# A fused two-layer trunk: attention from the first chunk to the last, with the other products in one even sequence

## The chip, the core and the metric

The kernel runs on one core of a Trainium2 chip. A core has a matrix engine (TensorE, PE in the profile; its weight loads are shown apart as PEld), three engines for element-wise work (VectorE or DVE, ScalarE or ACT, GpSimd or POOL), and SyncE (SP), which here issues nearly all DMA transfers between the device's memory and the core's own. Each engine takes its instructions in one fixed order; where one needs another engine's result, it waits at the head of its engine's queue, and what stands behind it waits too. The metric is the time of one execution on the device in microseconds (us), lower is better.

## The reference, cut to what matters

Two layers over a sequence of 2048 tokens with 1024 channels. Layer A is a pooling mixer; layer B is the attention that the change is about. Cut to layer B:

```python
kv_in = rms_norm(x, kv_norm)
k_all, v_all = jnp.split(kv_in @ w_kv, 2, axis=-1)
k_sh = rms_norm(split_heads(k_all), k_norm); v_sh = split_heads(v_all)
h = rms_norm(x, b_norm[j])
q, z = jnp.split(h @ b_w_in[j], 2, axis=-1)
q = rms_norm(split_heads(q), b_q_norm[j])          # 16 heads of 64
o = stick_breaking_attention(q, k_sh, v_sh)        # a[t,s] = beta[t,s] * prod_{s<i<t} (1 - beta[t,i]), s < t
x = x + (o * jax.nn.silu(z)) @ b_w_out[j]
x = x + (p[i] @ ple_w[i]) * jax.nn.sigmoid(x @ ple_gate_w[i])
```

beta is the sigmoid of the scaled logits. The product over the tokens between s and t is a scan along the keys, so attention is causal and has no softmax. The products of layer B outside attention are z (1024 to 1024), the output projection, the gate and the small per-layer embedding.

## The kernel before

Tokens are cut in four chunks of 512. The first `with` block computes layer A and q, k and v of layer B for chunks 0 to 3 in turn, and leaves q, k, v and the residual x2 in device memory. Every fp32 number that goes through a matmul is held as a pair, a rounded part and the rest, and a product of two pairs is three matmuls (high by high, high by low, low by high). The halves of x2 are kept in memory too (x2p), for chunks 0 to 2; those of chunk 3 are still on the core when they are wanted.

The second `with` block is attention with the rest of layer B woven in. Its work is a list of slots `(c, h, kc)`: query chunk c, head h, key chunk kc. The list goes through c = 3, 2, 1, 0, for each c through 16 heads, for each head through kc = c down to 0: 64, 48, 32 and 16 slots. Each slot has four steps, one per 128 queries in `front` and one per 128 keys in `turn` and `gather`, 640 steps in all:

- `front`: two matmuls for the logits (L790, L791), a sigmoid on ACT (L794), and the scan on DVE (L799 where kc = c, which is the diagonal and has 128 to 512 keys; L802 elsewhere, always 512).
- `turn`, six steps later: up to four transposes (L815), a cast on ACT (L818) and the low half on DVE (L819).
- `gather`, eight steps later: two matmuls with v (L827, L828). After a head's last one its 64 rows are copied and added (L832, L833); after every second head four ACT instructions add the ends (L839) and POOL multiplies by the stored z gate (L840).

`begin` loads q, k and v of the next slot at the first step of each slot; q, k and v share ten buffers of the pool `io`. The order of slots is written out by hand; within it the framework's planner fixes each engine's order by the program's order and its own estimate of times. `keep_in_program_order` pins an instruction behind all that was written before it on its engine.

The other products are a generator, the filler, that is advanced by a rate at every step; each `next` gives one 128x512 matmul (`piecewise`, L856, L858, L860). `gate_z(c)` makes z of one chunk (8 output tiles of 24 matmuls) and stores silu(z) (DVE L889, ACT L891, POOL L892, store L893). `post(c)`, called the rest below, is the output projection (L913 to L916), the gate, the embedding and the final store (L935 to L948); it needs all heads of chunk c. `pair_up` turns a finished pair of heads into its two halves (L868, L869), which `post` multiplies. Beside attention of chunk 3 run the z of chunks 3, 2, 1, 0; beside chunk 2 the rest of chunk 3; beside chunk 1 that of chunk 2; beside chunk 0 that of chunk 1. Last, without attention, comes the rest of chunk 0. The rate is set anew at each joint of chunks:

```python
rate = POSTZ / 64.0 - AHEAD * LAG_T / 256.0        # beside chunk 3
rate = POST / (64.0 * c3 - 2 * LAG_G)              # beside chunk c3 - 1
```

which is 2.91, 2.51, 3.94 and 9.19 pieces a step; the second form is spent 16 steps before its chunk's last.

Of the kernel before, what the change touches and what calls it, by code (L numbers as in the profile page):

```python
# [34 lines left out]
def trunk_kernel(ctx, tc, x, p, a_norm, a_w_in, a_w_group, a_scale, a_w_out, kv_norm, w_kv,  # L35
# [28 lines left out]
    x2p = [[dram.tile([P, 2, W5], F32, name=f"x2p{s}_{o}") for o in range(KT)] for s in range(NSUB - 1)]  # L64
# [114 lines left out]
    with ExitStack() as st:  # L179
# [316 lines left out]
        def run_g(s, b, wg, wl):  # L496
# [13 lines left out]
            for k in range(2):  # L510
# [4 lines left out]
                if s + 1 < NSUB:  # L515
                    nc.sync.dma_start(out=x2p[s][o], in_=f(pr))
# [231 lines left out]
    with ExitStack() as st:  # L748
# [16 lines left out]
        kcount = [0]  # L765

# [55 lines left out]
        def gather(st, kt):  # L822
# [6 lines left out]
            if st["last"] and kt == 3:  # L829
                half, os, c, h2 = st["h"] % 2, st["os"], st["c"], st["h"] // 2  # L830
                mine, other = slice(half * HD, (half + 1) * HD), slice((1 - half) * HD, (2 - half) * HD)
                A.copy(out=os[mine], in_=po[other])  # L832
                V.tensor_tensor(out=os[mine], in0=po[mine], in1=os[mine], op=ALU.add)  # L833
                if half:
                    zt = t2.tile([P, W5], F32, tag="zt", name="zt", bufs=1)
                    nc.sync.dma_start(out=zt, in_=zd[c][h2])
                    for j in range(4):
                        js = slice(j * P, (j + 1) * P)
                        A.activation(out=os[:, js], in_=os[:, js], func=AF.Identity, bias=ends[c][:, h2, j : j + 1])  # L839
                    G.tensor_tensor(out=os, in0=os, in1=zt, op=ALU.mult)  # L840
                    outs[c].append(os)

        tail = [0]
# [9 lines left out]
        def piecewise(ps, units, acts, c0):  # L853
            n = len(acts)
            for kt in range(n):
# [4 lines left out]
                T.matmul(ps, wst(units, kt, 1, c0), acts[kt][:, 0], start=False, stop=(kt == n - 1))  # L860
                yield

        def pair_up(c):

            if len(ogs[c]) < len(outs[c]):
                os = outs[c][len(ogs[c])]
                pr = pair("og")
                A.copy(out=pr[:, 0], in_=os)  # L868
                V.tensor_tensor(out=pr[:, 1], in0=os, in1=f(pr[:, 0]), op=ALU.subtract)  # L869
                ogs[c].append(pr)  # L870

        def gate_z(c):

            xs = chunk[c]["x2"] if c == NSUB - 1 else []
            for o in range(len(xs), KT):
                pr = pair("xz")
                nc.sync.dma_start(out=f(pr), in_=x2p[c][o])
                xs.append(pr)
# [5 lines left out]
            for o in range(KT):  # L884
                wz = early.pop("w") if "w" in early else stored(wzd[o])
                ps = dense()
                yield from piecewise(ps, wz, xs, 0)
                zr = t2.tile([P, W5], F32, tag="tmp", name="zr", bufs=4)
                V.tensor_tensor(out=zr, in0=ps, in1=rb, op=ALU.mult)  # L889
                sg = t2.tile([P, W5], F32, tag="tmp", name="sgz", bufs=4)  # L890
                A.activation(out=sg, in_=zr, func=AF.Sigmoid)  # L891
                G.tensor_tensor(out=zr, in0=zr, in1=sg, op=ALU.mult)  # L892
                nc.sync.dma_start(out=zd[c][o], in_=zr)  # L893
                if c == 0:
                    pair_up(NSUB - 1)

        POSTZ = 8 * 24
        POST = 8 * 24 + 8 * 30 + 9

        def post(c):  # L900
# [4 lines left out]
            while len(og) < 8:  # L905
                pair_up(c)
            for o in range(KT):
# [7 lines left out]
                A.copy(out=pr[:, 0], in_=xr)  # L915
                G.tensor_tensor(out=pr[:, 1], in0=xr, in1=f(pr[:, 0]), op=ALU.subtract)  # L916
                x3.append(pr)
            pt_ = []
# [8 lines left out]
            yield  # L927
            late = []
            for o in range(KT):
# [5 lines left out]
                A.activation(out=sg, in_=ps, func=AF.Sigmoid)  # L935
                pl = dense()
                yield from piecewise(pl, wl, pt_, 0)
                V.tensor_tensor(out=sg, in0=pl, in1=sg, op=ALU.mult)
                (V if tail[0] else G).tensor_tensor(out=sg, in0=sg, in1=f(x3[o][:, 1]), op=ALU.add)
                V.tensor_tensor(out=sg, in0=sg, in1=f(x3[o][:, 0]), op=ALU.add)  # L940

                def finish(o=o, sg=sg):
# [12 lines left out]
                if c:  # L955
                    pair_up(c - 1)
                yield
            late.pop()()
# [106 lines left out]
```

## Time and profile before

| | us |
|---|---|
| median of 3 runs | 2773.11 (2772.43 to 2773.38) |
| the profiled execution | 2771.59 |
| its span, first to last instruction | 2768.5 |
| first logits of attention | at 1364.04 |
| end of attention's last matmul | at 2660.84 |

The span is what the profile's times are counted in. An engine's busy time is the union of its instructions. A line of a group gives the source line, engine, operation, output and inputs, shapes and count, then busy time and the mean in nanoseconds of one, then idle time before it and what ended that. A line of a table by stretches gives the stretch and its length, then the busy time and count of PE, PEld, DVE, ACT and POOL, the granted clock of TensorE as a share of the full one, the mean busy share of the DMA engines, and their GB/s; for one source line alone it has only the engines which that line runs on.

### The profile page before, as it was taken

To read this page: it belongs to the slowest core of one execution; us is meant where nothing else is said; L and a number is where in the kernel's file an instruction comes from. 1 tells how busy PE (TensorE), PEld (TensorE's weight loads), DVE (VectorE), ACT (ScalarE), POOL (GpSimd) and SP (SyncE) were. 2 spreads that over 40 slices of the span, in tenths; PEclk is the share of its full clock that TensorE was granted. 3 is DMA by queue.
4 is the path that set the end of the run, shared out by engine and by line. 5 is a ranking of instruction groups with operands and counts; after the bars stand their busy time and mean duration, and the time that the engine had idled before them with its cause. 6 is when DMAs were issued, how large, how long until landed. Compare 5 with 4: busy or idle time off the path is not lost. (4 is left out here: it accounts for less than half of the span.)

```text
span 2768.5 us, 39557 instructions
## 1 busy us (share of the span) xinstructions
PE 2725.8 (98%) x13715; PEld 2259.8 (82%) x13715; DVE 1962.6 (71%) x2573; ACT 1385.6 (50%) x2801; POOL 871.2 (31%) x695
## 2 busy tenths in 40 slices
PE   9999999999999999999999999999999999999999
PEld 7888888888888888888878888887878778878877
DVE  6767535655357544565499999999999998996642
ACT  5445532445234552345356566566666666564431
POOL 2575338542475325753121111111110011102120
PEclk9999999999999999999999999999999999999999
DMA  8655695647946489444678565556555565668765
GB/s 290 237 189 177 218 335 195 224 147 254 342 151 231 162 255 310 134 149 169 194 251 284 173 218 171 164 168 189 162 160 166 181 191 186 199 185 265 240 206 160
DMA packets 335835, 573.21 MB, mean 207 GB/s; under 512 B 32462, under 2 KB 166638, under 8 KB 335636
## 3 DMA queue, kind: packets, MB, share of 16 engines
q1 hardware_dynamic: 330186, 563.03, 62.3%
q10 hardware_dynamic: 5450, 7.66, 0.9%
q8 instruction: 108, 1.77, 0.3%
q14 instruction: 91, 0.75, 0.1%
HBM read 430.01 MB, written 132.19 MB: 203 GB/s over the span
## 5 line engine op out<-in xcount | busy, mean ns | idle before, releaser
L536 PE MATMUL psd<-wpair,x 128*128 128x512 f32 x2304 | 543.8, 393 | 0.0
L818 ACT CAST at<-psa 128x512 fp32r<-128x512 f32 (+3 forms) x640 | 333.6, 522 | 403.1 <-PE psa L815 397.5
L802 DVE TENSOR_TENSOR_SCAN pp<-kap,pp,zeros 128x512 f32<-128x512 f32 x384 | 507.9, 1324 | 4.9 <-ACT kap L794 4.4
L536 PEld LDWEIGHTS psd<-wpair,x 128*128 128x128 f32 x2304 | 428.1, 188 | 86.2
L819 DVE TENSOR_TENSOR at<-psa,at 128x512 fp32r<-128x512 f32 (+3 forms) x640 | 379.9, 595 | 76.5 <-ACT at L818 73.2
L815 PE MATMUL psa<-ident,pp 128*128 128x128 f32 x2176 | 346.1, 274 | 19.3 <-DVE at L819 17.3
L794 ACT ACTIVATE kap<-psl 128x512 f32<-128x512 f32 (+3 forms) x640 | 344.7, 539 | 10.2 <-PE psl L791 9.3
L815 PEld LDWEIGHTS psa<-ident,pp 128*128 128x128 f32 x2176 | 263.8, 140 | 95.2 <-DVE at L819 38.4
L790 PE MATMUL psl<-kk,qa 128*128 128x512 f32 (+3 forms) x640 | 280.3, 438 | 0.4 <-ACT kap L794 0.4
L828 PE MATMUL pso<-at,vv 128*128 128x512 f32 (+3 forms) x640 | 235.5, 368 | 0.0
L827 PE MATMUL pso<-at,vv 128*128 128x512 f32 (+3 forms) x640 | 233.7, 365 | 0.7 <-ACT at L818 0.6
L791 PE MATMUL psl<-kk,qb 128*128 128x512 f32 (+3 forms) x640 | 233.7, 365 | 0.0
L799 DVE TENSOR_TENSOR_SCAN pp<-kap,ahead 128x128 f32<-128x128 f32 (+3 forms) x256 | 226.7, 887 | 6.0 <-ACT kap L794 4.7
L131 PE MATMUL psd<-xp,wpair 128*128 128x512 f32 x512 | 201.7, 395 | 1.9 <-ACT xp L269 1.4
L132 PE MATMUL psd<-xp,wpair 128*128 128x512 f32 x512 | 200.5, 392 | 0.0
L133 PE MATMUL psd<-xp,wpair 128*128 128x512 f32 x512 | 200.0, 391 | 0.0
L113 DVE SCALAR_TENSOR_TENSOR wpair<-wraw,gains,wpair 128x512 fp32r<-128x512 f32 x192 | 170.4, 908 | 37.5 <-ACT wpair L112 36.1
L892 POOL TENSOR_TENSOR zr<-zr,sgz 128x512 f32<-128x512 f32 x32 | 62.2, 1944 | 383.0 <-ACT sgz L891 305.6
L108 POOL TENSOR_TENSOR wpair<-wraw,wpair 128x512 fp32r<-128x512 f32 x99 | 146.0, 1489 | 60.2 <-ACT wpair L106 60.2
L112 ACT ACTIVATE wpair<-wraw,gains 128x512 fp32r<-128x512 f32 x192 | 134.7, 719 | 58.9 <-PE psd L536 32.9
L827 PEld LDWEIGHTS pso<-at,vv 128*128 128x128 f32 x640 | 120.2, 188 | 27.4 <-ACT at L818 1.6
L828 PEld LDWEIGHTS pso<-at,vv 128*128 128x128 f32 x640 | 120.3, 188 | 24.7
(211 smaller groups left out, 5396.4 us busy)
## 6 DMA issues: line engine op xcount, KB each, us to landing
kk<-kd SPq DMA_DIRECT2D x320, 128.0 KB
vv<-vd SPq DMA_DIRECT2D x160, 256.0 KB
wraw<-in_w_kv_dram SPq DMA_DIRECT2D x128, 256.0 KB
wpair<-wzd SPq DMA_DIRECT2D x64, 512.0 KB
wpair<-wod SPq DMA_DIRECT2D x64, 512.0 KB
wpair<-wgd SPq DMA_DIRECT2D x64, 512.0 KB
wpair<-wu SPq DMA_DIRECT2D x48, 512.0 KB
wpair<-wi SPq DMA_DIRECT2D x36, 512.0 KB
```

What stands on the lines that cost most here:

```text
L131: T.matmul(ps, wst(units, kt, 0, c0), acts[kt][:, 0], start=(begin and kt == order[0]), stop=False)
L536: T.matmul(pss2[i], ck["x2"][kt][:, xh, tk], wst(ws, kt, wh, 0, W5), start=(kt == 0 and xh == 0 and wh == 0), stop=(kt == KT - 1 and wh == 1))
L790: T.matmul(ps[:, :w], qa[:, qs], kk[:, :w], start=True, stop=False)
L791: T.matmul(ps[:, :w], qb[:, qs], kk[:, :w], start=False, stop=True)
L794: A.activation(out=kp[:, r0:], in_=ps[:, :w], func=AF.Sigmoid, scale=-1.0)
L799: V.tensor_tensor_scan(out=pp[:, r0:][:, ::-1], data0=kp[:, r0:][:, ::-1], data1=ahead[:, r0:][:, ::-1], initial=1.0, op0=ALU.mult, op1=AL ...
L802: V.tensor_tensor_scan(out=pp[:, ::-1], data0=kp[:, ::-1], data1=zeros.to_broadcast([P, W5]), initial=st["carry"][j], op0=ALU.mult, op1=AL ...
L815: T.transpose(pt[:, j * P : (j + 1) * P], pp[:, r0 + kt * P : r0 + (kt + 1) * P], ident)
L818: A.copy(out=at[:, 0, cs], in_=pt[:, cs])
L819: V.tensor_tensor(out=at[:, 1, cs], in0=pt[:, cs], in1=f(at[:, 0, cs]), op=ALU.subtract)
L827: T.matmul(po[:, cs], vv[:, kt, :], at[:, 0, cs], start=(st["diag"] and kt == 0), stop=False)
L828: T.matmul(po[:, cs], vv[:, kt, :], at[:, 1, cs], start=False, stop=(st["last"] and kt == 3))
```

## The change

1. The slots go through c = 0, 1, 2, 3. The first q and k that are loaded early are those of chunk 0.
2. There is one filler for the whole of attention: z of chunks 0, 1, 2, the rest of chunk 0, z of chunk 3, the rest of chunks 1 and 2. The rest of chunk 3 comes last, without attention. Its rate has two values, one for diagonal steps and one for the others, worked out over all 640 steps so that 20 pieces remain at the end.
3. All four chunks' x2 halves are stored and loaded again: those of chunk 0 before attention begins, those of chunks 1 and 2 behind the last output tile of the z before, those of chunk 3 at the end of the rest of chunk 0.
4. Late issue: `soon(k, fn)` puts an instruction k steps later in the program. It is used for the copy, the sum and the gate after a head, for the sigmoid and the gate of z, for the halves in `pair_up` and `post`, and for the gate's sigmoid and last sum in `post`; most of the ACT instructions among these are pinned in program order (`stay`). After attention everything is issued at once again.

The diff, cut to its core:

```diff
-    x2p = [[... for o in range(KT)] for s in range(NSUB - 1)]
+    x2p = [[... for o in range(KT)] for s in range(NSUB)]
...
+    def load_x2(c, o):
+        pr = pair("xz")
+        nc.sync.dma_start(out=f(pr), in_=x2p[c][o])
+        return pr
...
-                early["q"] = load_q(NSUB - 1, 0)
-                early["k"] = [load_k(NSUB - 1, 0), load_k(NSUB - 2, 0)]
+                early["q"] = load_q(0, 0)
+                early["k"] = [load_k(0, 0), load_k(0, 1)]
+                early["x"] = [load_x2(0, o) for o in range(KT)]
...
+        due, now, tail = [], [0], [0]
+        def soon(k, fn):
+            if tail[0]:
+                fn()
+                return lambda: None
+            item = (now[0] + k, len(due), fn)
+            due.append(item)
+            def force():
+                if item in due:
+                    due.remove(item)
+                    fn()
+            return force
...
+        def stay(ins):
+            return ins if tail[0] else tc.keep_in_program_order(ins)
...
-                A.copy(out=os[mine], in_=po[other])
-                V.tensor_tensor(out=os[mine], in0=po[mine], in1=os[mine], op=ALU.add)
+                soon(1, lambda: stay(A.copy(out=os[mine], in_=po[other])))
+                soon(2, lambda: V.tensor_tensor(out=os[mine], in0=po[mine], in1=os[mine], op=ALU.add))
+                if half:
+                    soon(3, gated)
+                    soon(6, lambda: outs[c].append(os))
...
+                follows = o == KT - 1 and c < 2
+                def behind(kt):
+                    early.setdefault("x", []).append(load_x2(c + 1, kt))
+                yield from piecewise(ps, wz, xs, 0, behind if follows else None)
...
+                def silu(o=o, zr=zr):
+                    sg = t2.tile([P, W5], F32, tag="tmp", name="sgz", bufs=4)
+                    stay(A.activation(out=sg, in_=zr, func=AF.Sigmoid))
+                    G.tensor_tensor(out=zr, in0=zr, in1=sg, op=ALU.mult)
+                    nc.sync.dma_start(out=zd[c][o], in_=zr)
+                    gates.add((c, o))
+                soon(1, silu)
...
-        def beside(c):
-            if c < NSUB - 1:
-                yield from post(c + 1)
-                return
-            for cz in range(c, -1, -1):
-                yield from gate_z(cz)
+        def beside():
+            for c in range(NSUB - 1):
+                yield from gate_z(c)
+            yield from post(0)
+            yield from gate_z(NSUB - 1)
+            for c in range(1, NSUB - 1):
+                yield from post(c)
...
-        for c in range(NSUB - 1, -1, -1):
+        for c in range(NSUB):
...
-        rate = POSTZ / 64.0 - AHEAD * LAG_T / 256.0
+        SPARE = 20
+        nd = sum(4 for c, h, kc in slots if kc == c)
+        on_diag = 3.1
+        off_diag = (4 * POSTZ + 3 * POST - SPARE - AHEAD * LAG_T - on_diag * nd) / (4 * len(slots) - nd + LAG_G)
...
-            owed += rate + (AHEAD if n < LAG_T else 0)
+            owed += on_diag if i < len(slots) and slots[i][2] == slots[i][0] else off_diag
+            owed += AHEAD if n < LAG_T else 0
...
+        settle()
+        pair_up(NSUB - 1)
+        settle()
+        for _ in filler:
+            settle()
         tail[0] = 1
-        for _ in post(0):
+        for _ in post(NSUB - 1):
             pass
```

More of the change, by code (lines that the diff above doesn't have):

```diff
@@ L867, in pair_up @@
                 pr = pair("og")
-                A.copy(out=pr[:, 0], in_=os)
-                V.tensor_tensor(out=pr[:, 1], in0=os, in1=f(pr[:, 0]), op=ALU.subtract)
+                stay(A.copy(out=pr[:, 0], in_=os))
+                soon(1, lambda: V.tensor_tensor(out=pr[:, 1], in0=os, in1=f(pr[:, 0]), op=ALU.subtract))
                 ogs[c].append(pr)
         def gate_z(c):
[L874 to L878, printed above, removed]
+            xs = early.pop("x")
             ps = (psl if "w" in early else psa).tile([P, 4, P], F32, tag="psl" if "w" in early else "psa", name="psar")
@@ L914, in post, with halves @@
                 pr = pair("x3")
[L915 to L916 removed]
+                def halves(pr=pr, xr=xr):
+                    stay(A.copy(out=pr[:, 0], in_=xr))
+                    G.tensor_tensor(out=pr[:, 1], in0=xr, in1=f(pr[:, 0]), op=ALU.subtract)
+                made = soon(1, halves)
                 x3.append(pr)
+                if o < 2 and c < NSUB - 1:
+                    pair_up(c + 1)
             pt_ = []
@@ L927, in post @@
             yield
+            made()
             late = []
```

65 lines of the change are left out of this document (32 added, 33 removed).

## The prediction

> **What bounds the kernel now.** I read the page first: the shares of the engines.
>
> ```profile
> span 2768.5 us, 39557 instructions
> ## 1 busy us (share of the span) xinstructions
> PE 2725.8 (98%) x13715; PEld 2259.8 (82%) x13715; DVE 1962.6 (71%) x2573; ACT 1385.6 (50%) x2801; POOL 871.2 (31%) x695
> ```
>
> PE looks busy throughout. But a matmul is shown from its start to a modelled end, and ends overlap the next starts (a case stands below), so 98% may hide a PE that works below its pace. So next comes the table of stretches, cut where a new chunk's first logits (L790) start: chunks 3, 2, 1, 0, and then the end without attention.
>
> ```profile
> 1364.00:1864.60 500.60, 496.73 (x2706) 414.03 (x2705) 472.02 (x564) 298.94 (x598) 79.06 (x44) 1.00 0.64 204
> 1864.60:2219.60 355.00, 344.12 (x1917) 283.31 (x1916) 344.22 (x434) 226.80 (x468) 38.93 (x25) 1.00 0.55 172
> 2219.60:2480.80 261.20, 255.09 (x1409) 212.38 (x1408) 235.47 (x305) 156.25 (x338) 34.39 (x24) 1.00 0.60 190
> 2480.80:2660.80 180.00, 174.24 (x940) 145.55 (x939) 121.90 (x190) 91.92 (x220) 32.15 (x24) 1.00 0.76 241
> 2660.80:2768.50 107.70, 100.88 (x461) 82.51 (x460) 24.90 (x36) 17.90 (x32) 11.59 (x9) 0.99 0.55 176
> ```
>
> After the colon pair and the length come PE, PEld, DVE, ACT, POOL, the clock, the DMA share and GB/s. Attention takes 2660.8 - 1364.0 = 1296.8 us for 256 + 192 + 128 + 64 = 640 steps. The clock is full throughout, so it plays no part. DVE is at 94, 97, 90 and 68%: the stages have different limits. That is the opening for an even mix.
>
> The same table for the products' first matmul (L856) alone shows stretches that have almost none:
>
> ```profile
> 1863.50:1876.50 13.00, 0.00 (x0) 0.19 (x1) 1.00 0.60 186
> 2204.10:2232.30 28.20, 0.00 (x0) 0.01 (x1) 1.00 0.52 164
> 2466.80:2493.60 26.80, 0.79 (x2) 0.38 (x2) 1.00 0.56 171
> 2639.10:2660.80 21.70, 1.81 (x5) 0.94 (x5) 1.00 0.59 188
> ```
>
> They are the joints between chunks, 89.7 us in sum, in which PE has attention's own work only. The rate leaves 16 steps empty before each joint and 8 steps drain after it.
>
> Then the stretches between the joints, whole heads of chunks 3, 2, 1 and 0 (144, 144, 96 and 32 steps), for all engines, and in the second fence for L856:
>
> ```profile
> 1428.80:1706.90 278.10, 278.10 (x1526) 232.98 (x1525) 263.95 (x317) 168.93 (x339) 42.04 (x23) 1.00 0.70 222
> 1893.30:2160.20 266.90, 262.42 (x1464) 218.29 (x1462) 260.77 (x328) 170.06 (x351) 32.12 (x20) 1.00 0.53 168
> 2249.20:2450.90 201.70, 199.77 (x1099) 167.52 (x1097) 180.17 (x232) 118.57 (x255) 29.18 (x20) 1.00 0.61 195
> 2517.00:2615.10 98.10, 98.10 (x524) 83.41 (x522) 62.29 (x94) 46.14 (x109) 20.14 (x15) 1.00 0.80 255
> ```
>
> ```profile
> 1428.80:1706.90 278.10, 55.37 (x140) 26.32 (x140) 1.00 0.70 222
> 1893.30:2160.20 266.90, 47.01 (x118) 22.17 (x118) 1.00 0.53 168
> 2249.20:2450.90 201.70, 49.03 (x123) 23.12 (x123) 1.00 0.61 195
> 2517.00:2615.10 98.10, 38.24 (x96) 18.07 (x96) 1.00 0.80 255
> ```
>
> Every product matmul comes in threes (L856, L858, L860), so the stretches hold 420, 354, 369 and 288 of them, and steps of 1.931, 1.853, 2.101 and 3.066 us. What one costs PE is its start to the next start:
>
> ```profile
> 2717.11 0.60 PE L945 MATMUL psao<-ident,sg 128*128 128x128 f32 x4
> 2717.46 0.47 PE L856 MATMUL psdt<-x,wpair 128*128 128x512 f32 x1
> 2717.77 0.39 PE L858 MATMUL psdt<-x,wpair 128*128 128x512 f32 x1
> 2718.00 0.39 PE L860 MATMUL psdt<-x,wpair 128*128 128x512 f32 x1
> ```
>
> 2717.77 to 2718.00 is 0.23 us for a product; four transposes and a product, 2717.11 to 2717.77, take 0.66, so a transpose takes 0.108.
>
> **The sum for PE.** In the stretches of chunks 3 and 0 PE is busy all the time, so what is left after the products is attention's own need. Chunk 3: (278.1 - 420 x 0.23) / 144 = 1.260 us a step. Chunk 0, all steps on the diagonal, with about 24 transposes of rest: (98.1 - 66.2 - 2.6) / 32 = 0.916. So a step off the diagonal takes (4 x 1.260 - 0.916) / 3 = 1.375. Chunk 2 then needs (0.916 + 2 x 1.375) / 3 = 1.222, chunk 1 1.146. One z is 192 products, 44.2 us; one rest is 432 products and 40 transposes, 103.7 us or 0.2346 for each of its 442 pieces. All of it: 256 x 0.916 + 384 x 1.375 + 4 x 44.2 + 3 x 103.7 = 1250 us. The attention part took 1296.8, so 47 us are the most that any order can win.
>
> **The sum for DVE.** Its own work per step is what stands in the stretch less the products' share, from the groups of the chunk 3 stretch and, in the second fence, of the chunk 0 stretch:
>
> ```profile
> L889 DVE TENSOR_TENSOR zr<-psd,rb 128x512 f32<-128x512 f32 x18 | 12.0, 666 | 0.6 <-issue 0.6
> ...
> L869 DVE TENSOR_TENSOR og<-os,og 128x512 fp32r<-128x512 f32 x2 | 1.3, 676 | 0.0
> ```
>
> ```profile
> L940 DVE TENSOR_TENSOR sg<-sg,x 128x512 f32<-128x512 f32 x5 | 4.5, 907 | 6.9 <-POOL sg L939 6.9
> L913 DVE TENSOR_TENSOR xr<-psd,xr 128x512 f32<-128x512 f32 x6 | 4.1, 677 | 0.6 <-issue 0.6
> L938 DVE TENSOR_TENSOR sg<-psd,sg 128x512 f32<-128x512 f32 x5 | 3.4, 674 | 0.8 <-PE psd L860 0.8
> L869 DVE TENSOR_TENSOR og<-os,og 128x512 fp32r<-128x512 f32 x4 | 2.6, 676 | 2.6 <-ACT og L868 2.6
> L925 DVE TENSOR_TENSOR ple<-psap,ple 128x512 fp32r<-128x512 f32 x2 | 1.3, 666 | 0.0
> ```
>
> In chunk 0's stretch 15.9 us go with 288 products, 0.055 each; a z with one og per 24 products comes to 2 x 0.67 / 24 = 0.056, the same. Own work a step: chunk 3 (263.95 - 13.3) / 144 = 1.740; chunk 2 260.77 / 144 - 0.135 = 1.676; chunk 1 1.877 - 0.211 = 1.666; chunk 0 1.947 - 0.495 = 1.452.
>
> **The change, part by part.** (1) Order and rate. 3.1 pieces go to a diagonal step, and (768 + 1326 - 20 - 24 - 3.1 x 256) / (640 - 256 + 8) = 3.205 to the others, with 24 extra in the first six steps. The chunks mix them to 3.1, 3.153, 3.170 and 3.179. PE a step (0.23 a piece in chunks 0 and 1, 0.233 and 0.2346 in 2 and 3): 1.629, 1.871, 1.961, 2.006. DVE a step (0.055 a piece): 1.62, 1.84, 1.85, 1.915. In chunks 0 and 1 both are level. Chunk 2's old stretch was so too: PE 1.222 + 354 / 144 x 0.23 + 0.02 = 1.81, DVE 1.811, and a step took 1.853, that is 1.023 of the greater. I add that 2.3% in chunks 0 and 1, and nothing in 2 and 3, since chunk 3's old stretch held PE at 278.10 of 278.10 with DVE at 95%. Sum: 64 x 1.667 + 128 x 1.914 + 192 x 1.961 + 256 x 2.006 + 24 x 0.23 = 1247 us. Then 8 draining steps, at the old end's 21.7 / 16 = 1.36 us, 10.9, and the 20 pieces kept back, 4.7, under which the last head's chain lies. Attention 1263 against 1297: -34 us. The part after it stays at 107.7: the same 432 products, for chunk 3 in place of 0.
>
> (2) Eight more stores of x2 halves, in chunk 3's first layer, and eight more loads, 512 KB each: 4.2 MB each way. Cover: in the window 1050 to 1130, in the midst of that, PE is full:
>
> ```profile
> 1050.00:1130.00 80.00, 80.00 (x355) 66.23 (x354) 39.46 (x50) 20.47 (x38) 53.16 (x51) 1.00 0.75 260
> ```
>
> I take nothing; at the window's 260 GB/s with a share of 0.75, some 347 GB/s at a full share, the 4.2 MB would be 12 us if the cover were gone. The next z's halves are loaded behind each product step of the last column, 21 pieces or 6 steps ahead; z of chunk 3 gets its own as the halves before it are freed. Nothing, with 2 us as the upper end for one late first load.
>
> (3) Late issue: copies, sums and gates of attention go one to six steps back in ACT, DVE and POOL order, so that none stands at the head of its queue with its input not made. Gain: nothing to the 1% idle in chunk 1's old stretch, some 2.5 us over that chunk; loss: os and the logits' output bank are held two steps longer, nothing to 2 us in chunk 0, where a head has only four steps. I take nothing.
>
> (4) SP. In chunk 0 every slot is a new head and needs seven loads, one round of which is (first and last row of seven; below it the longest wait of SP's queue in chunk 0, and the longest in chunk 3, with total, times and longest):
>
> ```profile
> 2514.62 0.45 SPq L152 DMA_DIRECT2D qa<-qd  x1
> ...
> 2518.36 0.53 SPq L165 DMA_DIRECT2D vv<-vd  x1
> ```
>
> ```profile
> SPq L152 <- PE psl L791: 34.8, 13, 5.4
> ```
>
> ```profile
> SPq L893 <- POOL zr L892: 103.8, 30, 5.8
> ```
>
> The round is 4.27 us long and starts when the q of two heads back is free (the wait on L791); a slot will last 4 x 1.667 = 6.7 us instead of 12.3. Now the z stores stand in that queue as well, and each holds it 103.8 / 30 = 3.46 us for POOL (up to 5.8). In chunk 3's old stretch these holds cost PE nothing, since a head had 16 steps. In chunk 0: between 0 and 8 x 3.46 = 27.7 us. The nearest row is the harmless one, but the cover is shorter; five steps, 8.3 us, less the round leave 4.1 for hold and landing. I take 0.5 a store, 4 us.
>
> Sum: -34 + 4 = -30. Against the profiled execution (2771.6 us, of which 2768.5 are span) 2741.6; against the median of 2773.1, 1.5 higher: 2743.
>
> **The rivals.** (a) PE reaches its pace in chunks 0 and 1 too, and SP costs nothing: no 2.3% on 104 and 240 us, so 2773 - 34 - 8 = 2731. For: 98.10 of 98.10 in chunk 0's old stretch. Against: DVE was at 63% there. (b) POOL slows DVE where it is level with PE. Rows:
>
> ```profile
> L802 DVE TENSOR_TENSOR_SCAN pp<-kap,pp,zeros x384: 1247/1273/2053, 1374.2 to 2483.0; 128x512 f32<-128x512 f32 x192
> ```
>
> ```profile
> L892 POOL TENSOR_TENSOR zr<-zr,sgz x32: 1283/2122/3772, 1373.8 to 1866.6; 128x512 f32<-128x512 f32 x32
> ```
>
> A scan can take 2053 ns instead of 1273, and the z gate 3772 instead of 1283. Chunks 0 and 1 get 24 z gates and 16 output gates: 40 x 0.78 = 31 us if each hits a scan that has no slack, half of it likely, since the old stretches hold some already: 2743 + 16 = 2759. [...] (c) The other side: the holds of SP fall ahead of each head's round in chunk 0, and PE waits for q and k. With the longest hold, 8 x 5.8 = 46: 2743 - 4 + 46 = 2785. It decides from (30 + 4) / 8 = 4.3 us a store. For: the 4.1 us of cover. Against: PE has no wait for a q or k load in the old chunk 0. (d) The change doesn't do what it says: the order on each engine is a planner's, by its own costs, and if that bunches the products again the joints stay: 2773.
>
> **How the numbers follow.** A measurement tells 0.2%, 5.5 us, from no change. The forecast, 2738 to 2751, has 0.55; (a) 0.12; (b) 0.16; (c) 0.12; (d) 0.05. Faster: forecast, (a) and nearly all of (b), 0.81; same: (d) and the top of (b), 0.06; slower: (c) and a little of (d), 0.13. The range leaves out (c), (d), the top of (b) and the bottom of (a): 2732 to 2768.
>
> **What would show it.** Right: L856 in every stretch of attention but the last 20 us; steps near 1.67, 1.91, 1.96 and 2.01 us in chunks 0 to 3; DVE near 97% in chunks 0 and 1 and 95% in 3; x2p halves landed before z needs them. Wrong: PE waiting for qa or kk in chunk 0 (c); scans with a mean well over 1.34 us there (b); stretches without L856 (d); an end after attention longer than 108 us.

## The result and the profile after

The changed kernel is slower: a median of 2800.93 us (five runs, 2795.68 to 2802.85) against 2773.11, a ratio of 1.0099 with a 95% interval of 1.0088 to 1.0110. The forecast was 2743, with slower at 0.13; the miss is 58 us. The page's head (busy time and share of the span):

```profile
span 2798.8 us, 39573 instructions
## 1 busy us (share of the span) xinstructions
PE 2741.5 (98%) x13715; PEld 2272.1 (81%) x13715; DVE 1960.5 (70%) x2573; ACT 1384.7 (49%) x2801; POOL 870.8 (31%) x695
```

PE has the same 13715 matmuls as before and still seems full, but it is busy 15.7 us longer. The table by stretches, cut at the first logits (now L821) of chunks 0, 1, 2, 3 and at attention's last matmul; columns as before, PE, PEld, DVE, ACT, POOL, clock, DMA share, GB/s:

```profile
1367.00:1517.30 150.30, 127.70 (x638) 100.56 (x636) 100.32 (x160) 76.79 (x188) 28.56 (x21) 0.93 0.81 232
1517.30:1765.20 247.90, 242.44 (x1321) 203.65 (x1321) 220.50 (x288) 148.81 (x326) 41.31 (x25) 0.99 0.76 229
1765.20:2148.60 383.40, 378.22 (x2087) 316.32 (x2086) 354.62 (x442) 230.81 (x475) 51.97 (x31) 1.00 0.62 190
2148.60:2682.40 533.80, 528.57 (x2890) 439.30 (x2889) 498.96 (x601) 315.97 (x631) 61.42 (x39) 1.00 0.54 164
2682.40:2798.80 116.40, 108.44 (x499) 89.01 (x497) 26.28 (x38) 19.46 (x35) 12.85 (x10) 0.99 0.60 190
```

Against the terms of the prediction's sum:

| stage | predicted us | measured us | miss |
|---|---|---|---|
| start of attention | 1364.0 | 1367.0 | +3.0 |
| chunk 0 (106.7 + 5.5 extra pieces + 4 for SP) | 116.2 | 150.3 | +34.1 |
| chunk 1 | 245.0 | 247.9 | +2.9 |
| chunk 2 | 376.5 | 383.4 | +6.9 |
| chunk 3 with the draining steps | 524.4 | 533.8 | +9.4 |
| the part without attention | 112.4 | 116.4 | +4.0 |
| span | 2738.5 | 2798.8 | +60.3 |

More than half of it is in chunk 0. Four of its eight stretches of eight steps, PE alone, and in the second fence a stretch for the products' first matmul (now L891):

```profile
1382.40:1397.60 15.20, 13.80 (x81) 1.00 0.79 229
1418.30:1438.70 20.40, 16.80 (x79) 0.83 1.03 240
1457.90:1477.30 19.40, 16.53 (x77) 0.83 0.52 164
1496.20:1517.30 21.10, 16.00 (x78) 1.00 0.88 281
```

```profile
1486.30:1503.90 17.60, 0.00 (x0) 0.01 (x1) 1.00 1.01 320
```

The first shown lasts 15.2 us with the full clock. The next two show a granted clock of 0.83: 79 and 77 matmuls cost more busy time than 81 did. The last has the full clock and still counts 16.00 us for 78: a product is shown some 0.39 us long where the next one starts 0.23 us later, so matmuls that stand apart count for more. Only part of the extra busy time is the clock. And inside chunk 0 there are stretches without a product again, here 17.6 us: its products come in bursts of 24, one output tile, with eight steps of attention alone between. The waits of PE and, in the second fence, of SP's queue in chunk 0 (total, times, longest), then the DMA totals of the last stage beside products in the kernel before, and of chunk 0 after:

```profile
PE psa L846 <- DVE at L850: 15.5, 20, 2.4
PE psa L846 <- DVE pp L830: 2.6, 5, 0.8
...
PE psl L821 <- DMA kk<-kd: 1.1, 1, 1.1
```

```profile
SPq L934 <- POOL zr L933: 23.2, 6, 8.9
```

```profile
DMA packets 23007, 43.35 MB, mean 241 GB/s; under 512 B 2816, under 2 KB 7424, under 8 KB 22993
```

```profile
DMA packets 19851, 34.92 MB, mean 232 GB/s; under 512 B 2520, under 2 KB 7091, under 8 KB 19840
```

PE hardly waits for a load by name; it waits in attention's short chain, where the products that should fill it are not there. The stores of z hold SP 23.2 us, once for 8.9. The last two lines are the sum that the prediction never made: the old chunk 0 moved 43.35 MB in 180 us, the new one must move 34.92 MB in its 150, and in the 112 us forecast for it without SP's holds that would have been 312 GB/s. The row 2517.00 to 2615.10 of the prediction gives 255 GB/s at a share of 0.80, so 319 at a full share: by this estimate the forecast asked for 98% of every DMA engine without having said so. By chunk 0's own row, 232 GB/s at 0.81, a full share is 286, less than was asked for.

### The profile page after: what moved, and what is told of

Same layout as the page of the kernel before. It is cut to its first block, busy times and chain, and to the rows that moved or that the text cites. A ratio compares the mean times of both kernels' runs of the same rounds, so it can differ in the third digit from the quotient of the medians.

```text
span 2798.8 us, 39573 instructions
## 1 busy us (share of the span) xinstructions
PE 2741.5 (98%) x13715; PEld 2272.1 (81%) x13715; DVE 1960.5 (70%) x2573; ACT 1384.7 (49%) x2801; POOL 870.8 (31%) x695
## 5 line engine op out<-in xcount | busy, mean ns | idle before, releaser
L825 ACT ACTIVATE kap<-psl 128x512 f32<-128x512 f32 (+3 forms) x640 | 343.3, 538 | 34.4 <-PE psl L822 30.6
L821 PE MATMUL psl<-kk,qa 128*128 128x512 f32 (+3 forms) x640 | 284.1, 445 | 3.1 <-ACT kap L825 1.7
L830 DVE TENSOR_TENSOR_SCAN pp<-kap,ahead 128x128 f32<-128x128 f32 (+3 forms) x256 | 224.6, 882 | 10.7 <-ACT kap L825 9.4
L992 POOL TENSOR_TENSOR sg<-sg,x 128x512 f32<-128x512 f32 x24 | 35.3, 1471 | 361.8 <-DVE sg L991 343.4
L963 POOL TENSOR_TENSOR x<-xr,x 128x512 fp32r<-128x512 f32 x32 | 50.8, 1588 | 301.2 <-ACT x L962 301.2
L858 PEld LDWEIGHTS pso<-at,vv 128*128 128x128 f32 x640 | 121.1, 189 | 27.6 <-DVE os L875 1.1
```

The costliest lines, as they stand in the source:

```text
L821: T.matmul(ps[:, :w], qa[:, qs], kk[:, :w], start=True, stop=False)
L825: A.activation(out=kp[:, r0:], in_=ps[:, :w], func=AF.Sigmoid, scale=-1.0)
L830: V.tensor_tensor_scan(out=pp[:, r0:][:, ::-1], data0=kp[:, r0:][:, ::-1], data1=ahead[:, r0:][:, ::-1], initial=1.0, op0=ALU.mult, op1=AL ...
L858: T.matmul(po[:, cs], vv[:, kt, :], at[:, 0, cs], start=(st["diag"] and kt == 0), stop=False)
```

## The experiments

The first theory after the result was that bursts cost the time (the planner, rival d) and that late issue or late weights make them. Then came the loads themselves, and last SP's order. All chunk times below are from the trace of the named run. Most build on e2, so that the planner's order plays no part.

**e1: late issue undone.**

```diff
         def soon(k, fn):
-            if tail[0]:
+            if True:
                 fn()
                 return lambda: None
...
-            return ins if tail[0] else tc.keep_in_program_order(ins)
+            return ins
```

> The changed kernel without the late issue: copies, sums and gates stand where their inputs are written, and none is pinned. Theory plan (the order of TensorE's queue in chunk 0 bunches 24 products because the planner takes a head's q, k and v to be late) and theory loads (on the chip itself the seven loads of a head, held behind the z stores, set a slot of chunk 0): both expect chunk 0's 64 steps to stay near 150 us and the time within 6 us of the changed kernel's 2801. Theory late issue (the gate of z comes late, holds SP, and that bunches the products): chunk 0 falls to 110 to 120 us, the time to 2760 to 2770.

Measured 2817.39 us, ratio 1.0161 (1.0146 to 1.0177); chunk 0 takes 163.5 us. Late issue is a gain of some 16 us in this order, 13 of them in chunk 0; it is not the cause. The time lies outside both ranges expected. Two waits of PE in chunk 0 of e1 show its place: transposes wait 11.0 us for scans, where the changed kernel has 2.6.

```profile
PE psa L846 <- DVE pp L830: 11.0, 20, 1.0
...
PE pso L858 <- ACT at L849: 4.4, 10, 0.6
```

**e2: every matmul of the first 80 steps pinned in the order in which it is written** (of attention's pairs the first one), which spreads the products evenly, three or four a step.

```diff
+        def inorder(ins):
+            return tc.keep_in_program_order(ins) if now[0] < 80 else ins
...
-            T.matmul(ps[:, :w], qa[:, qs], kk[:, :w], start=True, stop=False)
+            inorder(T.matmul(ps[:, :w], qa[:, qs], kk[:, :w], start=True, stop=False))
...
```

> The changed kernel with every matmul of the first 80 steps pinned in the order in which the program writes them, so that no step has more than 4 products behind it (7 in the first six). All loads stay as they are. Theory plan: the loads are quick enough on the chip, so a step of chunk 0 goes from 2.35 to about 1.7 us, chunk 0 from 150 to 108 to 115 us, the time to 2760 to 2766, below the kernel before. Theory loads: TensorE now waits in its queue for q and k, a step stays above 2.2 us, the time within 10 us of 2801.

Measured 2789.11, 1.0060 (1.0045 to 1.0075): chunk 1 gained 9 us (238.9), but chunk 0 stayed at 152.2. So the bursts are not what costs chunk 0 its time: with them gone, PE waits openly. The time is 12 us below 2801, 2 more than theory loads allowed. PE's waits in chunk 0, two stretches of eight steps, and SP's queue ahead of the longest wait (start, length, what is issued):

```profile
PE psd L894 <- DMA wpair<-wzd: 31.0, 4, 15.1
PE psl L824 <- DMA kk<-kd: 1.7, 1, 1.7
```

```profile
1473.90:1504.80 30.90, 15.57 (x84) 0.78 0.85 279
1504.80:1518.60 13.80, 13.28 (x80) 1.00 0.71 221
```

```profile
1486.51 1.97 SPq L160 DMA_DIRECT2D kk<-kd  x2
1489.26 0.33 SPq L165 DMA_DIRECT2D vv<-vd  x1
1491.45 1.27 SPq L178 DMA_DIRECT2D xz<-x2p  x3
1492.77 0.94 SPq L172 DMA_DIRECT2D wpair<-wzd  x2
```

The weights of z (wzd) are issued behind the halves of x2 for the next z (xz), which are issued behind a head's q, k and v. Eight steps take 30.9 us where 13.8 are enough.

**e3 and e4: q and k stored head by head**, so that five transfers load a slot instead of seven (qa and kk in one piece); e4 adds e2's order.

```diff
-            nc.sync.dma_start(out=f(qa)[l * HD : (l + 1) * HD], in_=rows[:, l])
...
+        nc.sync.dma_start(out=f(qa), in_=qd[c][h].rearrange("l d t -> (l d) t"))
...
```

> The changed kernel with q and k kept in memory head by head, so that k and one of the two q tiles come as one whole transfer of 128 partitions: five loads for a head in place of seven, the same bytes. The planner's order then has 17 empty steps in chunk 0 in place of 33. Theory plan: chunk 0 falls by the share of the bunches that go, about half of 38 us, the time to 2778 to 2786. Theory loads: a round goes from 4.3 to about 3.2 us of issue and the slot of chunk 0 by some 1.1 to 2 us, 18 to 32 us in sixteen slots, the time to 2770 to 2783. The two do not differ much here; with the next run they do.

> Whole tiles and the written order of the first 80 steps together. Theory plan: no better than the written order alone by more than 5 us, 2755 to 2766. Theory loads: well below the written order alone, by 15 to 30 us, near 2770.

Measured 2783.83 (1.0039, 1.0024 to 1.0054) and 2781.36 (1.0024, 1.0013 to 1.0036). Chunk 0 falls to 130.4 and 132.4 us with the same bytes, at 270 and 274 GB/s, but attention starts at 1374.8 and 1376.9: the edit also splits the first layer's stores of q and k in two, and some 8 to 10 of the 20 us are given back there. e3 is in the range of theory plan; e4, 7.8 us below e2, is in neither.

**e5: z's weights loaded one output tile earlier**, on e2.

```diff
+                if o + 1 < KT:
+                    ahead_w.append(stored(wzd[o + 1]))
```

> The written order of the first 80 steps, and in z the weights of the next output are loaded where the present output's product begins, 24 pieces earlier than before. In the run with the written order alone TensorE waited 31.0 us for z weights in chunk 0, which SP issued 1.5 to 7 us ahead of their use. Theory late weights (SP gives them out too late, the DMA itself has room): that wait goes, chunk 0 falls from 152 to 112 to 120 us, the time from 2789 to 2750 to 2758. Theory bytes (the stage moves 35 MB, at 232 GB/s with a share of 0.81 the full rate would be 286 GB/s and 122 us): chunk 0 stays at 125 to 140, the wait moves to q and k, the time 2765 to 2780.

Measured 2791.15, 1.0066 (1.0046 to 1.0086): no gain. PE's waits for wzd fell from 31.0 to 13.5 us and others took their place (9.4 for the stored gate, 7.1 for the first layer's last v); chunk 0 151.6. Both theories had expected less. Late weights are a symptom here: with them loaded sooner, something else came late.

**e6: the z weights of chunk 0 loaded once instead of eight times**, on e2.

```diff
+                if c == 0:
+                    if o == 0:
+                        keepw = early.pop("w")
+                    wz = keepw
```

> The written order, and z of chunk 0 loads one output's weights once and uses them for all eight outputs: 7 MB less in chunk 0, no wait for weights there (it leaves seven eighths of these weights out). Both theories take the wait for weights away; theory bytes has 28 MB left, 98 us at 286 GB/s, less than TensorE's own 107. So chunk 0 at 107 to 116 us and the time near 2750 in both; if late weights is right this run equals the one with the weights one ahead, if bytes is right it is 12 to 25 us faster than that one.

Measured 2769.18, 0.9993 (0.9983 to 1.0004). With 27.6 MB instead of 35.6, chunk 0 takes 121.6 us, 30.6 less than in e2 and 30.0 less than in e5, which speaks for the bytes. But both theories had 107 to 116 us, and chunk 1 took 245.8 us for e2's 238.9, so 20 of the 30 us are left in the whole time.

**e7: q in two transfers of all 128 partitions instead of four of 64**, same bytes, on e2.

```diff
-        for l in range(2):
-            nc.sync.dma_start(out=f(qa)[l * HD : (l + 1) * HD], in_=rows[:, l])
-            nc.sync.dma_start(out=f(qb)[(1 - l) * HD : (2 - l) * HD], in_=rows[:, l])
+        whole = qd[c][h // 2]
+        for q_ in (qa, qb):
+            nc.sync.dma_start(out=f(q_), in_=whole[:, 0])
```

> The written order, and each head's two q tiles loaded as two whole transfers of 128 partitions in place of four of 64 (the same bytes and buffers; both tiles get the same rows, of two heads, so the logits are not the reference's). Theory late weights: SP has 2 issues, 1.1 us, less a slot and lanes free sooner, so weights come a little earlier; chunk 0 at 140 to 150 us. Theory bytes: no gain beyond what better packing gives, chunk 0 at 140 to 150 as well. A third theory, that the transfers of 64 partitions are slow for their bytes, expects 115 to 130 us and 2755 to 2768.

Measured 2770.34, 0.9988 (0.9977 to 0.9998). The DMA totals of chunk 0 in e2 and, in the second fence, e7:

```profile
DMA packets 20078, 35.55 MB, mean 234 GB/s; under 512 B 2549, under 2 KB 7128, under 8 KB 20068
```

```profile
DMA packets 19637, 35.64 MB, mean 275 GB/s; under 512 B 2103, under 2 KB 6661, under 8 KB 19626
```

The same 35.6 MB at 275 instead of 234 GB/s: 129.7 us, as the third theory had it, with a time 2 us above its range. So 22.5 us of what holds chunk 0 are how its loads are carried. Whether that is the half tile itself or the two issues fewer a head, e7 does not tell apart; e3 and e4, also with two issues fewer, go the same way: 270 GB/s for the changed kernel's 232, and 274 for e2's 234.

**e8 to e11: chunk 1 first, then 0, 2, 3.** z goes 1, 0, 2, then the rest of 1, z of 3, the rests of 0 and 2. e8 has 2.0 pieces a step in chunk 0; e9 pins the matmuls of the first 192 steps as well; e10 and e11 are e9 with 2.5 and 3.1 pieces.

```diff
-        for c in range(NSUB):
+        for c in ORD:
             for h in range(NH):
...
+            owed += alone if here[0] == 0 else on_diag if i < len(slots) and here[2] == here[0] else off_diag
```

> The changed kernel with attention in the order of chunks 1, 0, 2, 3 and z of chunks 1, 0, 2, and 2.0 pieces a step in chunk 0, where all slots are diagonal (the lost pieces go to the others; the planner orders as it likes). Chunk 0 now comes after its neighbours' loads have settled, and asks for fewer weights. Theory bytes: chunk 0's attention alone needs 1 MB a slot; with 2.0 pieces some 26 MB, 92 us, and DVE's own 1.45 x 64 = 93; chunk 0 at 95 to 110 us, chunk 1 at 245 to 255, the whole time 2755 to 2768. Theory late weights: chunk 0 is a stage of seven loads a slot again and weights come late again: 120 to 150 us, the time 2775 to 2800.

> The order 1, 0, 2, 3 of e8 with the matmuls of its first 192 steps (chunks 1 and 0) held in the order in which they are written, pieces 2.0 a step in chunk 0. Load theory: in e8 chunk 1 took 248.7 us, where 238.6 to 238.9 were seen in e2 and e7, and chunk 0 116.1 with products in bursts; spread evenly chunk 1 goes to 239 to 244 and chunk 0 stays at 112 to 118, so 2763 to 2770, and faster than both kernels. Rival, what is left is PE's and DVE's own pace in chunks 1 to 3: no change from e8, 2770 to 2774.

> As e9 with 2.5 pieces a step in chunk 0 instead of 2.0. Load theory: 32 pieces more in chunk 0, 7.4 us of PE, and as many fewer in the others; chunk 0 has room for some of them (PE's need at 2.0 pieces is 64 x 1.376 = 88 us against 116 measured), so chunk 0 grows by 0 to 7 us and the rest shrinks by 7: 2759 to 2768. Rival, chunk 0 is held by its loads alone whatever the pieces: it grows by what the weights' 1 MB more takes, some 4 us, and the total falls by 3.

> As e9 with 3.1 pieces a step in chunk 0, the rate of the changed kernel, but with chunk 0 second. Load theory: the same bytes per step as in the changed kernel, so chunk 0 takes 125 to 150 us again though it is not the first. Rival, chunk 0 is slow because it is the first, with the transfers of the layer before it still under way and empty queues: as second it takes 107 to 115 us, near PE's need of 64 x 1.629 = 104, and the total is 2752 to 2760.

| run | median us | ratio to before (95%) | chunk 1 | chunk 0 | chunk 2 | chunk 3 |
|---|---|---|---|---|---|---|
| e8 | 2771.92 | 1.0000 (0.9991 to 1.0010) | 248.7 | 116.1 | 383.9 | 538.9 |
| e9 | 2777.77 | 1.0023 (1.0013 to 1.0033) | 255.6 | 116.0 | 384.6 | 538.9 |
| e10 | 2786.78 | 1.0050 (1.0038 to 1.0063) | 253.5 | 122.8 | 392.3 | 535.5 |
| e11 | 2774.13 | 1.0007 (0.9998 to 1.0016) | 251.2 | 122.7 | 382.9 | 533.7 |

e8 lies between its two theories, e9 and e10 missed. Order pinned, chunk 1 got slower: PE waits 15.8 us for z's weights in the two chunks of e9, and SP is held 64.3 us by 22 z stores there. e10's chunk 2 is 7.5 us longer than in any other run. Its granted clock there is 0.98 where the others have 1.00, some 6 us of the 392.3, and one wait for k takes 2.9 us; what brings the clock down in this run is not known. e11 answers its question in between: at the changed kernel's rate chunk 0 takes 122.7 us as the second, not the 150 of the first and not the 107 to 115 of the rival. But the x2 halves for the next z are then loaded in chunk 1, so it has 28.7 MB, not 35.6; that needed e13 to e17.

**e12: no pieces kept back for after the last step** (`SPARE = 0` for 20).

> The changed kernel with SPARE 0 instead of 20: no pieces are kept for after the last step. The end after attention took 116.4 us, 8.7 more than before. Theory: that is 449 products there instead of the 419 of before, 30 x 0.23 = 6.9 us of work moved, and 1.7 us of waiting for the last head's chain; with none kept back the end shrinks by about 4.6 us, attention grows by as much, and the waiting for the chain grows by 0 to 5: 2799 to 2806. Rival, the pieces kept back are a loss: 2792 to 2797.

Measured 2803.20, 1.0109 (1.0093 to 1.0124): the end shrinks by 4.5 us to 111.9, chunk 3 grows by 5.5 to 539.4. The work is only moved.

**e13 and e14: the stores of z on GpSimd's own queue**, in the changed kernel and on e2.

```diff
-                    nc.sync.dma_start(out=zd[c][o], in_=zr)
+                    nc.gpsimd.dma_start(out=zd[c][o], in_=zr)
```

> The changed kernel with the stores of z (L934) put on GpSimd's own DMA queue, right behind the multiplication that makes z, so that none stands in SP's queue. In the changed kernel SP was held 29.6 us by 7 of these stores from 1397 to 1550 us. Theory SP: these holds push back the loads of q, k, v and of weights behind them, and chunk 0 goes from 150 to 130 us or less, in all 2775 to 2785. Theory bytes: the 35 MB and the half-tile transfers set the pace whatever holds SP, the holds are time in which SP would have waited for free buffers anyway: chunk 0 stays at 142 to 152, in all 2793 to 2803. The prediction's own term for this was 4 us.

> As e13, with the matmuls of the first 80 steps held in written order as in e2 (2789.1 us, chunk 0 152.2). Theory SP: chunk 0 goes to 125 to 135 us and the total to 2762 to 2772. Theory bytes: 145 to 152 and 2783 to 2790.

Measured 2789.19 (1.0061, 1.0046 to 1.0076), chunk 0 145.0; and 2779.74 (1.0027, 1.0016 to 1.0038), chunk 0 140.9 against e2's 152.2. Both times fall between the two theories, and e13's chunk 0 is in the range of theory bytes. In chunk 0 SP's holds cost 5.3 us under the planner's order and 11.3 with the order pinned, in the whole time 11.7 and 9.4.

**e15 and e17: e2 and e14 without the x2 loads in chunk 0.**

```diff
-                follows = o == KT - 1 and c < 2
+                follows = o == KT - 1 and c == 1
+                if o == KT - 1 and not c:
+                    early["x"] = xs
```

> e2 without the eight loads of x2 halves for the z of chunk 1, 512 KB each, which SP issued in steps 46 to 54 of chunk 0; that z is computed from the halves of chunk 0 instead, so its part is left out of the result. In e2 the 8 steps from 48 on took 30.9 us against 13.0 to 15.6 in undisturbed ones, with one wait of 15.1 us for weights that were issued behind six of these loads. Theory: 4.2 MB at the stage's 238 GB/s are 17.6 us; these 8 steps go to 14 to 19 us, chunk 0 to 135 to 140, the total to 2772 to 2778. Rival, as in the prediction (2), that they are covered: nothing changes, 2787 to 2791.

> e2 with both edits, of e14 (z stores on GpSimd's queue) and of e15 (no x2 loads for chunk 1's z, which is computed from chunk 0's halves and so is left out). Chunk 0 took 152.2 us in e2, 140.9 in e14, 141.5 in e15. If the two are separate costs, chunk 0 takes 152.2 - 11.3 - 10.7 = 130 us and the total is 2767 to 2771; if both act on one and the same wait, it stays at 136 to 141, and the total at 2775 to 2780. Against e16 (chunk 0 second, neither x2 loads nor z stores of SP in it: 112.5 us with 25 products, 5.8 us, fewer) what is left over is the cost of being first.

Measured 2780.90 (1.0029, 1.0018 to 1.0039), chunk 0 141.5; and 2766.51 (0.9976, 0.9967 to 0.9986), chunk 0 131.3. The x2 loads cost 10.7 us with the stores in SP's queue and 9.6 without, the stores 11.3 and 10.2: two separate costs that add up. e15's time lies between its two theories. The rows of chunk 0 in e2, e6, e7, e14, e15 and e17, columns as in the first table:

```profile
1366.40:1518.60 152.20, 118.28 (x625) 100.14 (x623) 99.52 (x154) 74.41 (x183) 25.57 (x20) 0.89 0.77 234
1365.20:1486.80 121.60, 110.98 (x623) 94.22 (x622) 100.93 (x153) 74.60 (x183) 26.87 (x20) 0.99 0.76 227
1366.80:1496.50 129.70, 114.70 (x624) 96.46 (x623) 100.28 (x155) 74.44 (x183) 27.37 (x20) 0.96 0.88 275
1364.20:1505.20 141.00, 117.55 (x625) 99.67 (x623) 97.03 (x154) 74.55 (x183) 30.48 (x28) 0.90 0.82 254
1367.30:1508.80 141.50, 116.45 (x624) 98.54 (x623) 99.67 (x155) 74.21 (x183) 26.03 (x20) 0.93 0.75 222
1365.50:1496.90 131.40, 117.32 (x625) 99.15 (x624) 99.17 (x155) 75.00 (x184) 30.98 (x29) 0.92 0.81 239
```

**e16: e11 with the stores of z on GpSimd's queue**, the version that the above points to.

> e11 (order 1, 0, 2, 3, written order in the first 192 steps, 3.1 pieces a step in chunk 0; 2774.1 us, chunk 1 251.2, chunk 0 122.7) with the stores of z on GpSimd's queue. In e11 SP was held 67.5 us by 23 of them in chunks 1 and 0. Theory SP: chunk 1 goes to 239 to 244, chunk 0 to 107 to 115, the total to 2750 to 2762, faster than both kernels. Theory bytes: 2768 to 2776.

Measured 2758.33 us (2755.97 to 2762.18), ratio 0.9951 (0.9937 to 0.9966): faster than both kernels. The table of stretches of the profiled execution (the slowest of the four, 2762.18): chunks 1, 0, 2, 3 and the end; below it, three stretches of eight steps in chunk 0, PE alone.

```profile
1367.80:1612.20 244.40, 242.68 (x1338) 203.74 (x1337) 224.07 (x292) 150.23 (x325) 55.93 (x47) 1.00 0.81 251
1612.20:1724.70 112.50, 107.92 (x623) 92.83 (x622) 99.52 (x154) 73.14 (x183) 24.75 (x22) 0.98 0.82 239
1724.70:2109.50 384.80, 377.80 (x2083) 315.62 (x2082) 355.50 (x443) 232.81 (x481) 59.97 (x40) 1.00 0.64 198
2109.50:2643.20 533.70, 528.45 (x2890) 439.04 (x2888) 499.01 (x601) 316.38 (x631) 61.44 (x39) 1.00 0.54 164
2643.20:2759.90 116.70, 108.65 (x500) 89.17 (x498) 26.25 (x38) 19.57 (x35) 12.87 (x10) 0.98 0.60 189
```

```profile
1654.20:1667.30 13.10, 13.10 (x80) 1.00 0.82 261
1667.30:1680.30 13.00, 13.00 (x80) 1.00 0.82 255
1680.30:1693.90 13.60, 13.26 (x80) 1.00 0.88 238
```

**e18: the kernel before with its z stores on GpSimd's queue**, nothing else.

> The kernel before with nothing changed but the z stores on GpSimd's queue. e16 is 14 us faster than the kernel before. Theory: its gain comes from the even mix, the joints that went, and the stores only let chunk 0 and 1 keep pace; in the kernel before the z stores stand in chunk 3, where heads have 16 steps, so 2771 to 2775, no change. Rival: the stores in SP's queue cost the kernel before as well, and the gain is theirs: 2757 to 2766.

Measured 2772.45, 1.0001 (0.9992 to 1.0010). The stores cost the kernel before nothing; e16's gain is not theirs alone. No run puts late issue into the kernel before or takes it out of e16, so how much of the gain is the mix and how much late issue (16 us in e1) is not shown.

## Why the prediction was wrong

**What failed: in part (1) the 64 x 1.667 us of chunk 0, which are PE's and DVE's pace with nothing for its loads, and the small terms for loads in parts (4) and (2).** The order and rate were costed by PE and DVE, and SP by how long it takes to issue. What the loads themselves need was left out. Chunk 0 took 150.3 us against 116.2; that loads hold it under the planner's order too shows e3, where whole tiles bring it to 130.4. In written order it took 152.2, 36 more than forecast:

- Part (4), "0.5 a store, 4 us", measured 11.3 (e2 to e14) and 10.2 (e15 to e17), some 7 us too small; in the changed kernel's own order it is 5.3 in chunk 0 (e13). The harmless row that it leaned on was a chunk with 16 steps a head; the bounds of 0 and 27.7 did hold it. Rival (c) named a cause that is there, but it is less than a third of the 36 us and not where (c) looked: in the changed kernel PE waits for q and k only 1.1 us, and it is the weights behind them in the queue that are late (31.0 us in e2).
- Part (2), "nothing, with 2 us as the upper end", measured 10.7 and 9.6. The 12 us worked out there "if the cover were gone" came close, but for other loads of the same size: the cover was sought in the first layer, while the eight loads for chunk 1's z, put at nothing, fall into the last third of chunk 0, which has no cover.
- The rest, 131.3 - 112.2 = 19 us, is left with both gone. It is loads too, at least in part, as far as e6 and e7 show: from the same 152.2, 8 MB fewer bring 30.6 us and whole q tiles 22.5. How much of it is the place as the first is not settled. Between e17 and e16 chunk 0 falls from 131.3 to 112.5 us; 5.8 of that are the 25 extra pieces that the first chunk takes, but e16's chunk 0 also moves 26.9 MB for 31.5, so the other 13 may be place or bytes. The two are in part one thing: whichever chunk is first carries the first layer's last v. Of the issues in e17's chunk 0 these two are of that kind, 3 MB, and SP is held 9.8 us for v there. No run takes them out, so what they cost is open.

```profile
vd<-vv SPq DMA_DIRECT2D x4, 512.0 KB
vl<-vl SPq DMA_DIRECT2D x4, 224.0 KB
```

**Part (3), late issue**, taken at nothing with a gain up to 2.5 us, is worth 16 in this order (e1). The term was far too small, but this error works against the miss.

**Rival (d)** came partly true: products bunched again, in chunk 0 and the start of chunk 1, and the old joints did go. Bunching itself is worth 12 us by the medians and 7 by the profiled spans (e2), all in chunk 1. **Rival (b)** fell: in chunk 1 the full scans kept their mean, shown here before (all of them) and after.

```profile
L802 DVE TENSOR_TENSOR_SCAN pp<-kap,pp,zeros 128x512 f32<-128x512 f32 x384 | 507.9, 1324 | 4.9 <-ACT kap L794 4.4
L833 DVE TENSOR_TENSOR_SCAN pp<-kap,pp,zeros 128x512 f32<-128x512 f32 x63 | 83.6, 1328 | 5.1 <-ACT kap L825 5.0
```

1328 ns stands below the 1.34 us set for it, and DVE was at 67 and 89% in chunks 0 and 1, not 97.

**The 2.3% in part (1)** was not needed in chunk 1. With the products in written order (e2) its row is

```profile
1518.60:1757.50 238.90, 238.87 (x1336) 202.42 (x1334) 223.31 (x294) 151.00 (x332) 43.85 (x26) 1.00 0.78 235
```

which is PE's pace alone, 128 x 1.871 = 239.5 us, with DVE at 93%, as rival (a) had it for chunk 1. That the changed kernel's 247.9 lies near the 245.0 of the forecast is luck: 5.5 us too much for level engines stand against 9 us for the bursts, which had no term.

**Part (1) in chunks 2 and 3** was short by 6.9 and 9.4 us, nearly the same in most runs above, 1.8% each. The prediction added nothing here. The longest waits of PE in chunk 2, and in chunk 3, are for DVE:

```profile
PE psa L846 <- DVE at L850: 2.5, 5, 1.0
PE psao L999 <- DVE sg L993: 1.8, 1, 1.8
```

```profile
PE psa L846 <- DVE at L850: 2.6, 4, 1.7
PE psao L999 <- DVE sg L993: 1.3, 1, 1.3
```

All of PE's waits listed there make 4.9 and 4.7 us. The stretch of chunk 3 from which "nothing" was taken was 278 us without a wait, but it was no sample of the whole chunk. What is left, 2 to 5 us in each, I cannot place.

**The part after attention**, 107.7 + 4.7 = 112.4, came out at 116.4. The products' first matmul there, after and (second fence) before:

```profile
2682.40:2798.80 116.40, 59.39 (x150) 28.00 (x149) 0.99 0.60 190
```

```profile
2660.80:2768.50 107.70, 55.23 (x140) 26.04 (x140) 0.99 0.55 176
```

Ten more of each of three lines, 30 products, are 6.9 us; the prediction had 20, having taken the old part for a whole rest of 432, where it held 420. Most of the other part is a wait of 1.7 us of PE for DVE (sg) soon after attention; the old end had one of 0.6 us near there. As e12 shows, such pieces are moved, not lost.

**What was right.** PE's pace: 3.1 pieces and a diagonal step were worked out at 1.629 us, and e16's full stretches of eight steps last 13.0 us, 1.63. Chunk 1 keeps PE's pace in e2, and in e16, where as the first it has 24 pieces more, it takes 244.4 us for 239.5 + 5.5. With its loads out of the way chunk 0 comes to 112.5 with 198 products, 8% over PE's 104. The joints did go, and with chunk 1 first an even mix with late issue is a gain, but a small one: e16's attention takes 1275.4 us for the 1296.8 of before. Of these 21 us 9 go into the part behind it and 4 into a later start, so the span of its profiled execution is 9 us shorter; its median is 14 us lower, where 30 were forecast.

## What to carry to other kernels

Before work is moved into a stage, add up that stage's bytes and divide them by its new length: a stage that is shortened by a third needs its loads at half as much again the rate, which from a share of 0.8 comes to 1.2 (the old chunk 0 had 0.76 at 241 GB/s; the new one, of which 312 GB/s were asked, reached 0.81 at 232). Then walk the queue that issues its loads in order, and ask of each entry how long it holds those behind it now that the slot is shorter; where those have no slack, a store that waits for a slow engine belongs on that engine's own queue: the move took 11.3 us off chunk 0 from e2 to e14 (in the kernel before, where they had slack, it changed nothing: a ratio of 1.0001).

## What the hardware showed

Some pauses of PE came with half the clock. In chunk 0 of the changed kernel the granted clock was 0.50 in three stretches of 6.8 us, from 1416.7, 1437.2 and 1457.7 us. In the 3.4 us before them PE was busy 1.56, 1.27 and 1.92 us. The second with what stands before and behind it, and in the second fence e2, in the last 10 us of its wait of 15.1 us and behind it (PE alone):

```profile
1433.80:1437.20 3.40, 1.27 (x10) 1.00 1.05 325
1437.20:1444.00 6.80, 5.84 (x19) 0.50 1.02 208
1444.00:1450.80 6.80, 6.80 (x35) 1.00 1.02 259
```

```profile
1490.30:1504.00 13.70, 3.45 (x11) 0.50 0.91 314
```

PE was busy 127.7 us in chunk 0, where e16 needs 107.9 and 25 products, 5.8: 14 us more. The 20 us at half the clock can explain at most 10 of them; the others I put down to matmuls that stand apart, as said above. The granted clock of the kernel before was 1.00 in all four rows of attention, so they could not show it. In the row of e2 the half clock goes with one wait for a load, of 15.1 us; the changed kernel's longest listed wait of a matmul in chunk 0 is 2.4 us, so there it goes with short ones. Not every such pause is followed by it: from 1474.8 to 1478.2 us PE was busy 1.79 us, and the clock stayed at 1.00, in the 6.8 us behind it too. What brings the clock down is not shown.

Equal bytes took unequal time: 35.6 MB of chunk 0 went at 234 GB/s with q in half tiles of 64 partitions (e2) and at 275 in whole ones, with two issues fewer a head (e7).
